# Two-layer encoder trunk: one projection block ahead of layer 1's second half, and the second half's first convolution pair starts on VectorE's own taps

## The chip, the cores and the metric

The kernel runs on one core of a Trainium2 chip, in fp32. The metric is the device time of one launch in microseconds (us), taken as the median of several runs. A profile shows one execution. The engines are named as in the profile: PE (TensorE matmul), PEld (its weight loads), DVE (VectorE), ACT (ScalarE), POOL (GpSimd) and SP (SyncE, which issues most DMAs).

## The reference

The input x has 1024 tokens of 1024 features. Every layer is x = x + mixer(RMSNorm(x)).

```
layer 0: h = rmsnorm(x); projections of h feed an S5 state-space layer with GLU (A)
         and a multi-scale retention (B), each times its own SiLU gate;
         x1 = x + concat(A, B) @ w_out            # 2048 -> 1024 features
layer 1: h1 = rmsnorm(x1)
         a, b, g = h1 @ w_c                        # three times 1024 features
         u = a * sigmoid(b)
         c = causal depthwise conv of u, 31 taps per feature, plus bias
         z = silu(layernorm over features(c)) * silu(g)
         x2 = x1 + z @ w_out_c
out = rmsnorm(x2)
```

Only layer 0's closing projection and layer 1 matter here.

## The kernel before, in words

**Tiling.** Data lies transposed: features on the 128 partitions, tokens along the free dimension. The 1024 tokens are two halves h = 0 and 1 of 512, the 1024 features 8 blocks nb of 128. Nearly every operation works on a tile of 128x512. A matrix product in fp32 is made of three passes in a faster type (`mm3`, L200 to L202): both operands are split into a high and a low part, and a product over 8 input blocks is 24 matmuls. The projection of layer 0 (`w_out`) has 16 input blocks, so 48 matmuls for a block of output. Its output tile is `mm_wo`; DVE adds the residual at L1418 and the sum of squares for the next norm follows (`square_sum`, "s1").

**Weights.** `plan` writes down the order in which weight blocks are used. A block is loaded by DMA (`wf`), cast by ACT to its high part (`wh`, L189), and POOL or DVE subtracts to make the low part (`wl`, L190). Each of `wf`, `wh` and `wl` has three buffers. For blocks needed in both halves, the low part is kept in device memory and loaded again for the second half (`wload_again`, L166).

**Layer 1.** `h1(h)` makes the normalized input in slices `h1h`/`h1l` (L1437 to L1441). `ab(h)` computes for each block the product b (`mm_b`), its tanh on ACT (`sb`, L1456), the product a (`mm_a`), and on DVE the gated `u` (L1469). `conv(h, n2)` computes the convolution of the pair of blocks n2 and n2+1. Of its 31 taps, ACT and POOL make the first few: ACT multiplies (L1502, L1506; tiles `tp`, three buffers), POOL adds (L1507). Unless the pair is `late`, ACT copies that partial sum into the accumulator in PSUM (L1513, two buffers), and DVE adds the other taps one by one, alternating between the two blocks (L1534). For a `late` pair, DVE starts with a multiply (L1531) and adds the partial sum ahead of the last tap (L1521). For the later pairs a pilot mean is subtracted before the last tap (L1523). L1614 to L1620 add the last block's outputs and squares into `cs` and `cq`, whose sums over features PE makes (`cst`, L509). From them the layer norm follows. `w_out_c` is the closing projection (`mm_oc`), with DVE's residual add at L1696 (x_0_0, x_1_0 and so on: block, half).

**Order.** The program's stages have priorities (`self.at(n)`: a lower number comes first), and a few edges are written by hand (`issue_after`). A scheduler with a timing model then fixes the order of instructions on each engine at build time. On the chip every engine runs its own list in order and waits on semaphores. So an edit in one stage can change the order in all later stages. The convolution taps of the first half's last pair beyond certain numbers (`NORM_TAP`) are held behind the second half's norm sum (L440).

Of the kernel before, what the change touches and what calls it, by code (L numbers as in the profile page):

```python
# [35 lines left out]
G0 = 3  # L36
# [10 lines left out]
def un(ap):  # L47

    return ap.rearrange("p (c a) -> p a c", a=LANES)


def nat(ap):

    return ap.rearrange("p (a c) -> p a c", a=LANES)
# [16 lines left out]
class Trunk:  # L71
# [22 lines left out]
    def plan(self):  # L94

        A = self.A

        seq = [(A["w_u01"][nb] if nb < 2 else A["w_ab"][nb], f"u{nb}") for nb in range(8)]
        seq += [(A["w_ab"][nb], f"g{nb}") for nb in range(8, 24)]
        for p in range(4):  # L100
            seq += [(A["w_ab"][28 + p], f"k{p}"), (A["w_ab"][24 + p], f"q{p}")]

            if p == 0:
                seq += [(A["w_v"][j], f"v{p}_{h}_{j}") for h in range(2) for j in range(4)]
            elif p > 1:
                seq += [(A["w_v"][2 * p + i], f"v{p}_{i}") for i in range(2)]
        self.ws_d = self.dram.tile([2, 2, P, 2, KB, P], F32, name="ws_d")
        quad = lambda i, j, m: A["w_glu"][i, m, :, j]
        sums = lambda n, m: self.ws_d[n // 2, m, :, n % 2]
        glu = [q for m in range(2) for q in (quad(0, 0, m), quad(0, 1, m))]  # L110
        glu += [q(m) for q in (lambda m: sums(0, m), lambda m: sums(2, m), lambda m: quad(1, 1, m)) for m in range(2)]
        glu += [sums(n, m) for m in range(2) for n in (3, 1)]
        seq += [(q, f"glu{i}") for i, q in enumerate(glu)]

        def wo(h):
            return [q for nb in range(8) for q in ((A["w_out"][nb], f"wos{nb}_{h}"),
                                                   (A["w_out"][8 + nb], f"wor{nb}_{h}"))]

        def ab(h):
            return [q for nb in range(8) for q in ((A["w_c"][8 + nb], f"cb{nb}_{h}"),  # L120
                                                   (A["w_c"][nb], f"ca{nb}_{h}"))]
        def cg(h, nbs):
            return [(A["w_c"][16 + nb], f"cg{nb}_{h}") for nb in nbs]
        seq += wo(0) + wo(1)[:4] + ab(0) + wo(1)[4:] + cg(0, range(G0)) + ab(1) + cg(0, range(G0, 8))
        seq += cg(1, range(G0))
        seq += [(A["w_out_c"][nb], f"woc{nb}_{h}") for h in range(2) for nb in range(8)]
        self.wseq, self.wissued, self.wgot = seq, {}, 0
        self.low_load, self.early_low = {}, None
        self.wnames, self.lo_d = {n for _, n in seq}, {}
# [1133 lines left out]
    def layer0_back_and_layer1(self, st):  # L1263
        nc, A = self.nc, self.A
        v, gp = nc.vector, nc.gpsimd
        lp = self.lp
# [139 lines left out]
        accs = {}  # L1406

        def w_out(h, nbs):
            for nb in nbs:
                xt = lp.tile([P, HALF], F32, name=f"xr{nb}_{h}", tag="ld", bufs=2)  # L1410
                nc.sync.dma_start(xt[:], A["xT"][nb, :, hs(h)])
                ws = self.wnext(f"wos{nb}_{h}")
                wr = self.wnext(f"wor{nb}_{h}")
                ps = self.bank(f"mm_wo{nb}_{h}", aux=False)
                seq = [(ws, ys[h], kb) for kb in range(KB)] + [(wr, yr[h], kb) for kb in range(KB)]
                self.gemm_seq(ps[:], seq, self.hold if h and nb == 0 else None)
                t = lp.tile([P, HALF], F32, name=f"x1_{nb}_{h}", tag="ev", bufs=3)
                v.tensor_tensor(nat(t[:]), un(ps[:]), nat(xt[:]), op=ALU.add)  # L1418
                nc.sync.dma_start(self.x1_d[rows(nb), hs(h)], t[:])
                if (nb, h) == (1, 1):  # L1420
                    self.later = lambda t=t: self.square_sum(lp, t, 1, 1, "s1", accs)
                else:

                    bank = (lambda: self.bank("s1q_bank")) if (nb, h) == (7, 1) else None
                    self.square_sum(lp, t, nb, h, "s1", accs, bank)
# [24 lines left out]
        def ab(h):  # L1450
            for nb in range(8):
                wb = self.wnext(f"cb{nb}_{h}")
                pb = self.bank(f"mm_b{nb}_{h}", aux=False)
                self.gemm(pb[:], wb, hx[h])
                sg = lp.tile([P, HALF], F32, name=f"sb{nb}_{h}", tag="ev", bufs=3)
                tanh = nc.scalar.activation(nat(sg[:]), un(pb[:]), AF.Tanh, scale=0.5)  # L1456

                with self.tc.issue_after(tanh.ins) if h == 0 and nb == 0 else nullcontext():
                    wa = self.wnext(f"ca{nb}_{h}")
                    if (nb, h) == (0, 0):  # L1460
                        self.later()
                pa = self.bank(f"mm_a{nb}_{h}", aux=False)
                self.gemm(pa[:], wa, hx[h])
                u = lp.tile([P, PADW + HALF], F32, name=f"u{nb}_{h}", tag="u", bufs=5)
                if h == 0:
                    gp.memset(u[:, :PADW], 0.0)
                else:
                    nc.scalar.copy(u[:, :PADW], tail[:, nb, :])
                v.scalar_tensor_tensor(nat(u[:, PADW:]), nat(sg[:]), 1.0, un(pa[:]), op0=ALU.add, op1=ALU.mult)  # L1469
                if h == 0:  # L1470
                    nc.scalar.copy(tail[:, nb, :], u[:, HALF:])
                ub[h][nb] = u
# [20 lines left out]
        def conv(h, n2):  # L1493


            accs_, outs, us, s0s = [], [], [], []
            late = h == 0 and n2 == 0
            for nb in (n2, n2 + 1):
                u = ub[h][nb]
                with self.at(105000 + 100000 * h + 100 * nb):  # L1500
                    s0 = lp.tile([P, HALF], F32, name=f"tp{nb}_{h}_0", tag="tp", bufs=3)
                    nc.scalar.activation(s0[:], u[:, 0:HALF], AF.Identity, scale=cw[:, nb, 0:1],  # L1502
                                         bias=self.vec(V_CB, nb))
                    for k in range(1, NT[h]):
                        sk = lp.tile([P, HALF], F32, name=f"tp{nb}_{h}_{k}", tag="tp", bufs=3)
                        nc.scalar.mul(sk[:], u[:, k:k + HALF], cw[:, nb, k:k + 1])  # L1506
                        gp.tensor_tensor(s0[:], s0[:], sk[:], op=ALU.add)  # L1507
                us.append(u)
                s0s.append(s0)
                acc = ps_cv.tile([P, HALF], F32, name=f"cv{nb}_{h}", tag="cv")  # L1510
                if not late:
                    with self.at(105000 + 100000 * h + 100 * nb):
                        nc.scalar.copy(acc[:], s0[:])  # L1513
                accs_.append(acc)
                outs.append(opB.tile([P, HALF], F32, name=f"co{nb}_{h}", tag="B0"))
            for k in range(NT[h], CONV_K):
                for i, nb in enumerate((n2, n2 + 1)):
                    dst = outs[i] if k == CONV_K - 1 else accs_[i]
                    tap = us[i][:, k:k + HALF], cw[:, nb, k:k + 1]
                    if k == CONV_K - 1 and late:  # L1520
                        v.tensor_tensor(accs_[i][:], accs_[i][:], s0s[i][:], op=ALU.add)  # L1521
                    if k == CONV_K - 1 and n2 >= 4:
                        v.tensor_tensor(accs_[i][:], accs_[i][:], pilot[h][:], op=ALU.subtract)  # L1523

                    if (h, nb, k) == (1, KB - 1, CONV_K - 1):
                        self.last_tap = *tap, accs_[i], dst
                        continue

                    ahead = (h, n2) == (0, 6) and k >= NORM_TAP[i]
                    if k == NT[h] and late:  # L1530
                        v.tensor_scalar(dst[:], *tap, None, op0=ALU.mult)  # L1531
                        continue
                    with self.tc.issue_after(self.norm_first.ins) if ahead else nullcontext():
                        v.scalar_tensor_tensor(dst[:], *tap, accs_[i][:], op0=ALU.mult, op1=ALU.add)  # L1534
            cv[h][n2:n2 + 2] = outs
# [213 lines left out]
        with self.at(100000):  # L1749
            w_out(0, range(8))  # L1750
            h1(0)
        self.hold = {4: self.last_stat}
        with self.at(200000):
            w_out(1, range(2))
            with self.at(110000):
                ab(0)
            w_out(1, range(2, 8))
            h1(1)
        self.norm_first = self.last_sum
        with self.at(300000):  # L1760
# [166 lines left out]
```

## Time and profile before

| | us |
|---|---|
| three runs | 1144.89, 1144.9, 1146.61; median 1144.9 |
| profiled execution | 1147.62, span 1145.8, mean granted PE clock 0.994 |
| busy: PE | 1123.9 (98% of the span) |
| busy: DVE | 853.5 (74%) |
| busy: POOL, ACT | 657.7 (57%), 488.2 (43%) |
| layer 1's second half begins (`r_R` on PE, first half's norm) | 709.65 |
| the convolution norm's sums of the second half (`cst` on PE) | 1074.00 |

Times in the trace count from the start of the span. PE's busy share of 98% is an average; the prediction looks at single stretches. A group's line names source line, engine, operation and tiles; in brackets behind an instruction stands how long its engine was idle before it and what ended that idle time.

### The profile page before, as it was taken

The numbers are of one execution on the slowest core, as the hardware profiler recorded it, in microseconds if no ns is written. First come the engines' busy times: TensorE is split into PE (matmuls) and PEld (weight loads), VectorE is DVE, ScalarE is ACT, GpSimd is POOL, SyncE is SP. The second block draws the span as 40 slices with busy tenths as digits, with TensorE's granted clock in tenths as the row PEclk, the third lists the DMA queues.
The fourth block names the chain that finished last, engine by engine and source line by source line (L and its number), as shares of the span: only waits on it lengthen the run. The fifth ranks groups of instructions, "written<-read, shape, count | busy, mean of one in ns | idle before, by whom it ended". The sixth has DMA issues, their size and how long they took to land.

```text
span 1145.8 us, 17197 instructions
## 1 busy us (share of the span) xinstructions
PE 1123.9 (98%) x6286; PEld 983.4 (86%) x6286; DVE 853.5 (74%) x1464; ACT 488.2 (43%) x719; POOL 657.7 (57%) x448
## 2 busy tenths in 40 slices
PE   9999999999999999999999999999999999999997
PEld 7888888888887888999887888888888888888787
DVE  6975798888417369596669632599999899999844
ACT  6423232223223321414446423545545676444674
POOL 2059999999235445333475111589544568678563
PEclk9999999999999999999999999999999999999999
DMA  9345355555487766858998998666778655357865
GB/s 352 113 129 159 128 166 177 162 175 177 154 256 247 285 199 211 297 182 308 382 375 295 321 321 285 191 232 203 247 249 298 238 177 173 120 188 248 287 226 193
DMA packets 117638, 261.46 MB, mean 228 GB/s; under 512 B 10673, under 2 KB 42289, under 8 KB 116913
## 3 DMA queue, kind: packets, MB, share of 16 engines
q1 hardware_dynamic: 117552, 260.36, 67.5%
q8 instruction: 49, 0.80, 0.3%
q14 instruction: 37, 0.30, 0.1%
HBM read 181.48 MB, written 74.65 MB: 224 GB/s over the span
## 4 chain that ended last, share of the span: by engine, by line
PE 34%; DVE 8%; DMA 7%; issue 2%; POOL 2%; ACT 1%; SPq 1%; POOLq 0%; ACTq 0%; DVEq 0%
DVE cv L1534 5%; PE mm_wo L202 5%; PE mm_wo L201 5%; PE mm_wo L200 5%; PE mm_b L201 2%; PE mm_b L202 2%; PE mm_b L200 2%; PE mm_a L202 2%; PE mm_a L201 2%; PE mm_a L200 2%; PE mm_oc L202 2%; PE mm_oc L201 1%; PE mm_oc L200 1%; DMA wf_glu<-w_glu 1%; DMA t_d<-th 1%
## 5 line engine op out<-in xcount | busy, mean ns | idle before, releaser
L1534 DVE SCALAR_TENSOR_TENSOR cv<-u,convw,cv 128x512 f32<-128x512 f32 x398 | 273.0, 749 | 6.6 <-ACT cv L1513 4.6
L1507 POOL TENSOR_TENSOR tp<-tp,tp 128x512 f32<-128x512 f32 x64 | 83.2, 1299 | 33.7 <-ACT tp L1506 32.7
L200 PE MATMUL mm_g<-xh,wh_g 128*128 128x512 f32 x256 | 98.9, 386 | 0.0
L201 PE MATMUL mm_g<-xl,wh_g 128*128 128x512 f32 x256 | 97.3, 380 | 0.0
L202 PE MATMUL mm_g<-xh,wl_g 128*128 128x512 f32 x256 | 97.2, 380 | 0.0
L437 POOL TENSOR_TENSOR s1q<-s1q,s1q 128x512 f32<-128x512 f32 x12 | 17.6, 1466 | 79.8 <-ACT s1q L432 79.8
L1506 ACT ACTIVATE tp<-u,convw 128x512 f32<-128x512 f32 x64 | 45.4, 718 | 35.5 <-POOL tp L1507 34.8
L200 PEld LDWEIGHTS mm_g<-xh,wh_g 128*128 128x128 f32 x256 | 48.4, 189 | 8.6 <-issue 1.2
L202 PEld LDWEIGHTS mm_g<-xh,wl_g 128*128 128x128 f32 x256 | 48.4, 189 | 6.9
L201 PEld LDWEIGHTS mm_g<-xl,wh_g 128*128 128x128 f32 x256 | 48.4, 189 | 6.8 <-issue 0.4
L190 POOL TENSOR_TENSOR wl_v<-wf_v,wh_v 128x1024 fp32r<-128x1024 f32 x12 | 31.0, 2593 | 36.4 <-ACT wh_v L189 36.4
L190 POOL TENSOR_TENSOR wl_glu<-wf_glu,wh_glu 128x1024 fp32r<-128x1024 f32 x14 | 34.3, 2447 | 29.9 <-ACT wh_glu L189 29.9
L200 PE MATMUL mm_oc<-zh,wh_woc 128*128 128x512 f32 (+1 forms) x144 | 51.3, 367 | 0.0
L202 PE MATMUL mm_oc<-zh,wl_woc 128*128 128x512 f32 (+1 forms) x144 | 51.0, 357 | 0.1
L201 PE MATMUL mm_oc<-zl,wh_woc 128*128 128x512 f32 (+1 forms) x144 | 51.1, 356 | 0.0
L201 PE MATMUL mm_u<-xl,wh_u 128*128 128x512 f32 x128 | 48.4, 381 | 0.7 <-DVE xl L316 0.7
L200 PE MATMUL mm_wo<-ysh,wh_wos 128*128 128x512 f32 x128 | 48.9, 382 | 0.0
L200 PE MATMUL mm_g<-h1h,wh_cg 128*128 128x512 f32 x128 | 48.9, 382 | 0.0
L201 PE MATMUL mm_b<-h1l,wh_cb 128*128 128x512 f32 x128 | 48.7, 381 | 0.1
L202 PE MATMUL mm_b<-h1h,wl_cb 128*128 128x512 f32 x128 | 48.7, 380 | 0.0
L201 PE MATMUL mm_wo<-ysl,wh_wos 128*128 128x512 f32 x128 | 48.5, 379 | 0.0
L202 PE MATMUL mm_wo<-ysh,wl_wos 128*128 128x512 f32 x128 | 48.5, 379 | 0.0
(526 smaller groups left out, 3622.9 us busy)
## 6 DMA issues: line engine op xcount, KB each, us to landing
wf_g<-w_ab SPq DMA_DIRECT2D x16, 512.0 KB
wf_wos<-w_out SPq DMA_DIRECT2D x16, 512.0 KB
wf_wor<-w_out SPq DMA_DIRECT2D x16, 512.0 KB
wf_cb<-w_c SPq DMA_DIRECT2D x16, 512.0 KB
wf_ca<-w_c SPq DMA_DIRECT2D x16, 512.0 KB
wf_woc<-w_out_c SPq DMA_DIRECT2D x16, 512.0 KB
wf_v<-w_v SPq DMA_DIRECT2D x12, 512.0 KB
wf_cg<-w_c SPq DMA_DIRECT2D x11, 512.0 KB
```

The lines of the kernel that those rows point to most:

```text
L190: self.low_made = lo[i].tensor_tensor(wl[:].rearrange(fl)[:, c], wf[:, c], h.bitcast(F32), op=ALU.subtract)
L200: nc.tensor.matmul(ps, wh[:, kb, :], xh, start=start, stop=False, **more)
L201: nc.tensor.matmul(ps, wh[:, kb, :], xl, start=False, stop=False, **more)
L202: self.last_mm = nc.tensor.matmul(ps, wl[:, kb, :], xh, start=False, stop=stop, **more)
L437: nc.gpsimd.tensor_tensor(a, a, sq[:], op=ALU.add)
L1506: nc.scalar.mul(sk[:], u[:, k:k + HALF], cw[:, nb, k:k + 1])
L1507: gp.tensor_tensor(s0[:], s0[:], sk[:], op=ALU.add)
L1534: v.scalar_tensor_tensor(dst[:], *tap, accs_[i][:], op0=ALU.mult, op1=ALU.add)
```

## The change

Before layer 1's products of the first half, one output block of layer 0's projection for the second half is computed instead of two; the other seven follow after. The weight order follows, and the square sum that is deferred into `ab(0)` is that of block 0. Besides, the first convolution pair (blocks 0 and 1) of the second half is treated as `late`, as that of the first half already was.

```
-        seq += wo(0) + wo(1)[:4] + ab(0) + wo(1)[4:] + cg(0, range(G0)) + ab(1) + cg(0, range(G0, 8))
+        seq += wo(0) + wo(1)[:2] + ab(0) + wo(1)[2:] + cg(0, range(G0)) + ab(1) + cg(0, range(G0, 8))
...
-                if (nb, h) == (1, 1):
-                    self.later = lambda t=t: self.square_sum(lp, t, 1, 1, "s1", accs)
+                if (nb, h) == (0, 1):
+                    self.later = lambda t=t: self.square_sum(lp, t, 0, 1, "s1", accs)
...
-            late = h == 0 and n2 == 0
+            late = n2 == 0
...
-            w_out(1, range(2))
+            w_out(1, range(1))
             with self.at(110000):
                 ab(0)
-            w_out(1, range(2, 8))
+            w_out(1, range(1, 8))
```

## The prediction

> **What bounds the kernel now.** I read the windows by stage first, then the waits of TensorE, then the timelines of VectorE and TensorE around the last wait. The windows give, for each stretch, the length and the busy time of PE, PEld, DVE, ACT and POOL, then the granted clock, the DMA share and GB/s.
>
> ```profile
> 900.00:940.00 40.00, 40.00 (x195) 35.17 (x194) 32.77 (x56) 28.58 (x42) 24.58 (x19) 1.00 0.64 223
> 940.00:1066.00 126.00, 126.00 (x585) 110.13 (x584) 125.82 (x193) 65.77 (x98) 96.44 (x68) 1.00 0.59 191
> 1066.00:1078.00 12.00, 9.31 (x32) 6.17 (x31) 9.81 (x15) 6.75 (x9) 7.93 (x5) 0.86 0.77 278
> 1078.00:1146.00 68.00, 61.06 (x333) 53.63 (x331) 33.37 (x61) 42.72 (x67) 34.90 (x31) 0.97 0.63 214
> ```
>
> PE is full from 900 to 1066 us, one matmul each 126.00/585 = 0.215 us. DVE is full from 940 to 1066 (125.82 of 126.00) and idle for 40.00 - 32.77 = 7.2 us between 900 and 940. Only in the third row does PE lose time, and the waits of PE name it:
>
> ```profile
> PE cst L509 <- DVE cs L1616: 2.7, 1, 2.7
> ```
>
> This is the second half's convolution norm: its sums over features (`cst`) need the last taps of the last convolution pair, which DVE computes one after the other. The timeline of DVE up to that point (start, length, engine, line, operation, output<-inputs):
>
> ```profile
> 1062.51 2.06 DVE L1534 SCALAR_TENSOR_TENSOR cv<-u,convw,cv 128x512 f32<-128x512 f32 x3
> 1064.48 0.69 DVE L1523 TENSOR_TENSOR cv<-cv,pilot 128x512 f32<-128x512 f32 x1
> 1065.08 0.74 DVE L1534 SCALAR_TENSOR_TENSOR cv<-u,convw,cv 128x512 f32<-128x512 f32 x1
> 1065.74 0.74 DVE L1534 SCALAR_TENSOR_TENSOR co<-u,convw,cv 128x512 f32<-128x512 f32 x1
> 1066.39 4.70 DVE L1534 SCALAR_TENSOR_TENSOR cv<-u,convw,cv 128x512 f32<-128x512 f32 x6
> 1071.13 0.70 DVE L1523 TENSOR_TENSOR cv<-cv,pilot 128x512 f32<-128x512 f32 x1
> 1071.94 0.70 DVE L1614 TENSOR_TENSOR cvs_bank<-cv,cs 128x512 f32<-128x512 f32 x1
> 1072.55 0.74 DVE L1615 SCALAR_TENSOR_TENSOR co<-u,convw,cv 128x512 f32<-128x512 f32 x1
> 1073.20 0.74 DVE L1616 SCALAR_TENSOR_TENSOR cs<-u,convw,cvs_bank 128x512 f32<-128x512 f32 x1
> 1073.86 0.68 DVE L1696 TENSOR_TENSOR x<-mm_oc,x1l 128x512 f32<-128x512 f32 x1
> ```
>
> Taps that alternate between the two blocks of a pair take (1064.48 - 1062.51)/3 = 0.66 us each; taps of one block that follow each other directly, each needing the one before, take (1071.13 - 1066.39)/6 = 0.79 us. From the L1523 at 1071.13 to the start of `cst` are 2.87 us. PE over the same stretch:
>
> ```profile
> 1070.93 0.38 PE L202 MATMUL mm_oc<-zh,wl_woc 128*128 128x512 f32 x1
> 1074.00 1.79 PE L509 MATMUL cst<-cs,ones 128*128 128x512 f32 x2 [2.69 <-DVE cs L1616]
> 1075.58 1.92 PE L509 MATMUL cst<-cq,ones 128*128 128x512 f32 x2
> 1076.51 1.39 PE L200 MATMUL mm_oc<-zh,wh_woc 128*128 128x512 f32 x1
> 1077.72 0.39 PE L201 MATMUL mm_oc<-zl,wh_woc 128*128 128x512 f32 x1
> ```
>
> The last product before `cst` is block 3 of the closing projection on the first half's tokens, ended at 1070.93 + 0.38 = 1071.31; `mm_oc` starts again behind `cst`. The wait has a second price. The two pairs of `cst` and the matmul behind them take 1077.72 - 1074.00 = 3.72 us, and the same form in mid-kernel, at full clock, is much quicker:
>
> ```profile
> 709.65 1.02 PE L509 MATMUL r_R<-s1q,ones 128*128 128x512 f32 x2
> 710.11 0.78 PE L200 MATMUL mm_wo<-ysh,wh_wos 128*128 128x512 f32 x1
> 710.72 0.38 PE L201 MATMUL mm_wo<-ysl,wh_wos 128*128 128x512 f32 x1
> ```
>
> One pair and one matmul are 1.07 us there, so two pairs and one matmul would be 1.07 + (1.07 - 0.215) = 1.92 us: 1.8 us lost. The clock of that stretch agrees:
>
> ```profile
> 1075.00:1080.00 5.00, 5.00 (x15) 3.31 (x15) 1.44 (x3) 3.70 (x7) 3.55 (x2) 0.73 0.96 333
> ```
>
> So the end is set by PE up to 1071.3, by DVE's taps up to 1074.0, and by PE again. A microsecond at `cst` reaches the end in full unless the 6.9 us of PE idle in the last windows row absorb it; those lie behind further matmuls, at the very end.
>
> **The sum's base.** The profiled execution took 1147.62 us with a span of 1145.8 (1.8 outside it); the three runs have a median of 1144.9. I take differences from the trace and put them on 1144.9. Of a measurement of this kernel, about 0.2% (2.3 us) can be told from no change.
>
> **Part one: one projection block ahead of layer 1 of the second half.** It removes no work: 48 matmuls, 48 x 0.215 = 10.3 us of PE, with their weights' casts and DMAs, the add at L1418 and the deferred square sum, go behind `ab(0)`. The risk is at the transition.
>
> ```profile
> 718.06 0.38 PE L202 MATMUL mm_wo<-yr1h,wl_wor 128*128 128x512 f32 x1
> ```
> ```profile
> 724.68 1.54 DVE L1441 SCALAR_TENSOR_TENSOR h1l<-xn,vecs,h1h 128x512 fp32r<-128x512 f32 x2
> 738.76 0.69 DVE L1418 TENSOR_TENSOR x<-mm_wo,xr 128x512 f32<-128x512 f32 x1 [12.55 <-PE mm_wo L202]
> 739.37 0.68 DVE L1469 SCALAR_TENSOR_TENSOR u<-sb,mm_a 128x512 f32<-128x512 f32 x1
> ```
>
> Block 0 ends there on PE (the next matmul can follow at 718.06 + 0.215 = 718.3); the normalized input `h1l` of layer 1 is complete only at 726.2, and the second block now fills that gap. In the changed kernel's instruction order PE works there on three products at once (b0, a0, b1), 9 matmuls or 1.94 us for each of the eight slices of `h1`, while DVE delivers a slice each 1.39 us (two of the last operations above, an add and a rescale at about 0.7). So the gap stays covered: 0. If only b0 stood there, it would end at 726.2 + 3 x 0.215 instead of 718.3 + 24 x 0.215 = 723.5: 3.4 us of wait.
>
> What is late next is a weight. b0, a0 and b1 hold all three weight buffers; the cast of the next block's a-weights can start only when b0 is done, 59 matmuls behind 718.3, at 731.0.
>
> ```profile
> 731.04 1.06 ACT L189 CAST wh_cb<-wf_cb 128x1024 fp32r<-128x1024 f32 x1 [5.61 <-PE mm_b L201]
> 732.11 1.28 ACT L1456 ACT_TABLE_LOAD   x1
> 733.41 0.60 ACT L1456 ACTIVATE sb<-mm_b 128x512 f32<-128x512 f32 x1
> ```
> ```profile
> 732.17 2.37 POOL L190 TENSOR_TENSOR wl_cb<-wf_cb,wh_cb 128x1024 fp32r<-128x1024 f32 x1 [5.66 <-ACT wh_cb L189]
> ```
>
> ACT does `sb` first (0.60), then the cast (1.06), then POOL the low part (2.37): 731.25 + 0.60 + 1.06 + 2.37 = 735.3. PE wants it after 76 matmuls, at 734.7. Cost about 0.7 us with hand-overs; from 0 (the two orders swap by a little) to 1.5 (the table load of 1.28 falls into it too). The first `u` comes about 7 us earlier than 739.37, and with it the first taps; but in the order 28 taps of the first half's last pair still stand behind the second half's norm sum (L440), as before, and that sum comes with PE's last projection block. DVE waits for it with nothing else to do, so this head start is worth 0 at the far end.
>
> **Part two: the second half's first pair adds the other engines' taps last.** The accumulator no longer waits for ACT's copy (L1513); DVE begins with a multiply (L1531, which replaces one L1534) and adds ACT's and POOL's partial sum before the last tap, two L1521.
>
> ```profile
> 912.08 0.69 DVE L1469 SCALAR_TENSOR_TENSOR u<-sb,mm_a 128x512 f32<-128x512 f32 x1 [1.70 <-PE mm_a L202]
> 915.74 3.13 DVE L1534 SCALAR_TENSOR_TENSOR cv<-u,convw,cv 128x512 f32<-128x512 f32 x4 [2.98 <-ACT cv L1513]
> ```
> ```profile
> L1521 DVE TENSOR_TENSOR cv<-cv,tp x2: 690/695/700, 767.3 to 779.2; 128x512 f32<-128x512 f32 x2
> ```
>
> Gain: most of DVE's 7.2 us of idle before 940, about 6.7. Cost: two adds, 2 x 0.6 = 1.2 us of issue. But the partial sums of this pair now hold two of the three `tp` buffers until their L1521, where before the copy freed them at once. ACT's second tap of block 2 (L1506) therefore waits for a DVE instruction near 950, and then follow its chain of ACT taps and POOL adds,
>
> ```profile
> L1507 POOL TENSOR_TENSOR tp<-tp,tp 128x512 f32<-128x512 f32 x64 | 83.2, 1299 | 33.7 <-ACT tp L1506 32.7
> ```
>
> four of 1.30 us plus an ACT tap each, with POOL's other work between. By the order I place block 2's copy at about 964 with DVE out of work from about 956: 7.9 us idle. The gain of 6.7 is spent there, and at the last `u` of the half DVE is level with before,
>
> ```profile
> 993.30 0.68 DVE L1469 SCALAR_TENSOR_TENSOR u<-sb,mm_a 128x512 f32<-128x512 f32 x1
> ```
>
> give or take 4 us, since the POOL chain is worked out and not seen.
>
> **What decides: where the add of block 3 stands.** Before, DVE's add of the closing projection's block 3 (L1696 at 1073.86) stood behind L1616, so nobody waited for it. In the changed order it stands ahead of the last 5 taps of the last block, of L1523, L1614, L1615 and L1616. It waits for the product that PE ends at 1071.31, and DVE takes its instructions in order. So `cst` starts no earlier than 1071.31 + 0.60 (the add's issue) + 5 x 0.79 + 2.87 = 1078.7, against 1074.0: **+4.7 us**. PE cannot deliver earlier: it has no gap from 900 to there. DVE's own count comes to the same place: from 993.30 to L1616 there are 125 instructions instead of 120, and 12 taps in direct succession instead of 6, so 1074.0 + 5 x 0.66 + 6 x (0.79 - 0.66) = 1078.1. Its 4 us of uncertainty count only upward, since the product's end is the floor. With the 0.7 of the weight stall, which moves that floor: **+5.4 us**. The clock's 1.8 us after the wait were paid before and are paid again; they could shrink at most to 0.
>
> PE's wait at `cst` grows from 2.69 to about 7.4 us. The Trainium skill (TensorE: Matmul & The Clock Gate, Part 1) says that the clock halves after an idle window of some 3.4 us and returns after a busy one, with windows that run freely. This trace half agrees: half speed came after only 2.69 us, and lasted about 3.5. By that rule the longer wait costs the same one window, or two if the first one is only partly busy.
>
> Forecast 1144.9 + 5.4, and 0.2 for the skew of DVE's own arrival: **1150.5 us**.
>
> **Rivals.**
> *A longer block-2 chain* (chance 0.18): DVE is late at the add of block 3 by 3 to 5 us because POOL serves the norm's multiplications between the adds. For it: POOL is 96.44 of 126.00 us busy from 940 on. Time 1153.5 to 1155.5.
> *A second half-speed window* (0.10): the matmuls behind `cst` run another 3.5 us at half speed, 1.8 us more, about 1152.3. For it: the wait is nearly three times as long. Against: one dip per wait in the trace before.
> *Uncovered transition* (0.05): PE waits at 718 to 726, 3.4 us, about 1153.9. Against: three products interleaved.
> *Faster* (0.06): DVE keeps its 6.7 - 1.2 = 5.5 us and the add of block 3 costs it nothing; the wait of 2.69 and the slow clock of 1.8 go, less the weight's 0.7: 1144.9 - 3.8 = 1141.1. It decides when DVE reaches that add with its product long done, about 7 us before `cst` is wanted. Against it: the product ends at 1071.31, directly before `cst` on PE. It could come true only if the adds of the tail did not run in the order that the program gives.
> *No change* (0.05): the change reaches `cst` but the 6.9 us of idle in the last windows row absorb it, 1143 to 1147. Against: PE is the engine that is late there.
>
> **How the numbers follow.** The forecast itself has 0.56, with a range of its own from 1148.5 (no weight stall, half of the clock's loss gone) to 1152.5. The range takes in the chain and the clock: 1148.0 to 1155.5; outside are the two rivals below and a little above. Faster by over 0.2%: 0.06; within: 0.05; slower: 0.89.
>
> **What would show it.** In the changed profile the wait `cst` <- `cs` L1616 should read 7 to 8 us; the L1696 before the last five taps should show an idle time ended by PE `mm_oc`, or start right behind 1072; L1513 of block 2 should start at 960 to 968 and DVE idle some 8 us before it; the idle at 909 to 925 should be gone; PE should wait 0 to 1.5 us for a `wl_ca` near 734. I am wrong if `cst` starts before 1077, if PE waits at 718 to 726, or if the end doesn't move with `cst`.

## The result, and the profile after

The changed kernel takes 1157.95 us (median of 4 runs, 1156.26 to 1160.19), the kernel before 1145.76 beside it: a ratio of 1.0101, 95% interval 1.0084 to 1.0118, so some 12 us slower. The forecast had the sign, and half of the size. The profiled execution took 1157.04, its span is 1155.3.

Where one profile is set against another, a shift has to be taken out first. Up to layer 0's closing projection the program is the same, yet that stretch alone varies by several us from one execution to the next:

```profile
621.16 0.38 PE L200 MATMUL mm_wo<-ysh,wh_wos 128*128 128x512 f32 x1
```
```profile
616.77 0.38 PE L200 MATMUL mm_wo<-ysh,wh_wos 128*128 128x512 f32 x1
```

The first row is the first `mm_wo` before, the second the same matmul after: 4.4 us earlier without any edit. I therefore compare the way from this matmul to the start of `cst` and from there to the span's end. Before it is 1074.00 - 621.16 = 452.8 and 71.8 us; after, 1082.97 - 616.77 = 466.2 and 72.3. All of the loss, 13.4 us, lies ahead of `cst`, and the profiles' spans differ by less only because of the early stretch.

PE's waits behind 700 us, after, as far as they are new or longer (engine, line, who is waited for: total, times, longest):

```profile
PE cst L509 <- DVE cs L1616: 7.6, 1, 7.6
PE cm L1545 <- POOL csr L1543: 3.7, 1, 3.7
PE r_R L509 <- DVE s1q L440: 1.4, 1, 1.4
PE mm_b L201 <- DVE h1l L1441: 1.1, 1, 1.1
```
```profile
PE mm_a L202 <- POOL wl_ca L190: 0.3, 1, 0.3
```

`cst` waits 7.6 us instead of 2.7, as forecast. The wait of `cm`, the pilot mean of the second half, was not forecast, and of the last three only the 0.3 was. DVE's timeline after, the taps that follow a wait for a copy, and the end of the taps:

```profile
962.02 3.13 DVE L1534 SCALAR_TENSOR_TENSOR cv<-u,convw,cv 128x512 f32<-128x512 f32 x4 [6.20 <-ACT cv L1513]
...
1012.70 16.56 DVE L1534 SCALAR_TENSOR_TENSOR cv<-u,convw,cv 128x512 f32<-128x512 f32 x25 [4.83 <-ACT cv L1513]
...
1034.05 12.61 DVE L1534 SCALAR_TENSOR_TENSOR cv<-u,convw,cv 128x512 f32<-128x512 f32 x19 [1.43 <-ACT cv L1513]
...
1070.15 5.50 DVE L1534 SCALAR_TENSOR_TENSOR cv<-u,convw,cv 128x512 f32<-128x512 f32 x7
1075.56 0.68 DVE L1696 TENSOR_TENSOR x<-mm_oc,x1l 128x512 f32<-128x512 f32 x1
1076.16 3.91 DVE L1534 SCALAR_TENSOR_TENSOR cv<-u,convw,cv 128x512 f32<-128x512 f32 x5
```

The wait of 6.2 at block 2 is the one that was worked out from the `tp` buffers (7.9). The other two are new; the only such wait behind the last `u` before was this one:

```profile
1004.03 23.14 DVE L1534 SCALAR_TENSOR_TENSOR cv<-u,convw,cv 128x512 f32<-128x512 f32 x35 [0.18 <-ACT cv L1513]
```

And the add of block 3 (L1696 at 1075.56) shows no idle time at all: DVE comes to it straight from its taps. PE shows how close that is:

```profile
1075.01 0.38 PE L202 MATMUL mm_oc<-zh,wl_woc 128*128 128x512 f32 x1
1082.97 2.08 PE L509 MATMUL cst<-cs,ones 128*128 128x512 f32 x2 [7.58 <-DVE cs L1616]
```

The product ended at 1075.01 + 0.38 = 1075.39. So two chains meet there within 0.2 us, PE's (late by its own waits) and DVE's (late by the copies). Which of them costs the time cannot be read from this profile alone.

The new waits have one kind of source. ACT and POOL around the wait at 1012:

```profile
1003.03 0.72 ACT L1506 ACTIVATE tp<-u,convw 128x512 f32<-128x512 f32 x1 [0.62 <-POOL tp L1507]
1003.66 0.58 ACT L1481 ACTIVATE sgg<-mm_g 128x512 f32<-128x512 f32 x1
1007.83 0.72 ACT L1506 ACTIVATE tp<-u,convw 128x512 f32<-128x512 f32 x1 [3.59 <-POOL tp L1507]
1009.93 0.81 ACT L1502 ACTIVATE tp<-u,vecs,convw 128x512 f32<-128x512 f32 x1 [1.38 <-POOL tp L1507]
1010.65 1.03 ACT L166 CAST wh_cg<-wf_cg 128x1024 fp32r<-128x1024 f32 x1
1011.59 0.59 ACT L1481 ACTIVATE sgg<-mm_g 128x512 f32<-128x512 f32 x1
1012.08 0.58 ACT L1513 COPY cv<-tp 128x512 f32<-128x512 f32 x1
```
```profile
1013.03 1.27 POOL L1667 TENSOR_TENSOR co<-gl,co 128x512 f32<-128x512 f32 x1 [3.13 <-DMA gl<-gs_d]
1014.25 1.27 POOL L1543 TENSOR_TENSOR csr<-cs,co 128x512 fp32r<-128x512 f32 x1
```

The copy that DVE waits for stands in ACT's queue behind the next blocks' taps, which wait for POOL. And `csr`, for which PE waits, stands behind POOL's multiply of a gate (L1667) that waits for its DMA. In the kernel before, `csr` stands ahead of that multiply:

```profile
1007.52 1.30 POOL L1543 TENSOR_TENSOR csr<-cs,co 128x512 fp32r<-128x512 f32 x1
...
1013.62 1.28 POOL L1667 TENSOR_TENSOR co<-gl,co 128x512 f32<-128x512 f32 x1 [1.44 <-DMA gl<-gs_d]
```

The engines are hardly busier than before (DVE 854.4 us against 853.5, POOL 656.6 against 657.7, ACT 488.2 in both); their queues hold things in another order. No run shows why that DMA lands as late as it does.

### The profile page after: what moved, and what is told of

Its sections match the earlier page's. It is cut to its first block, busy times and chain, and to the rows that moved or that the text cites. A ratio compares the mean times of both kernels' runs of the same rounds, so it can differ in the third digit from the quotient of the medians.

```text
span 1155.3 us, 17207 instructions
## 1 busy us (share of the span) xinstructions
PE 1124.7 (97%) x6286; PEld 984.0 (85%) x6286; DVE 854.4 (74%) x1466; ACT 488.2 (42%) x717; POOL 656.6 (57%) x448
## 4 chain that ended last, share of the span: by engine, by line
PE 68%; DVE 10%; DMA 10%; issue 4%; POOL 3%; ACT 2%; SPq 2%; POOLq 0%; DVEq 0%; ACTq 0%
PE mm_wo L201 5%; PE mm_wo L200 5%; PE mm_wo L202 5%; PE mm_g L200 4%; PE mm_g L201 4%; PE mm_g L202 4%; DVE cv L1534 4%; PE mm_a L202 2%; PE mm_a L200 2%; PE mm_a L201 2%; PE mm_b L201 2%; PE mm_b L202 2%; PE mm_b L200 2%; PE mm_oc L202 2%; PE mm_oc L200 2%
## 5 line engine op out<-in xcount | busy, mean ns | idle before, releaser
L190 POOL TENSOR_TENSOR wl_v<-wf_v,wh_v 128x1024 fp32r<-128x1024 f32 x12 | 31.0, 2587 | 36.7 <-ACT wh_v L189 36.7
L190 POOL TENSOR_TENSOR wl_glu<-wf_glu,wh_glu 128x1024 fp32r<-128x1024 f32 x14 | 33.8, 2411 | 31.2 <-ACT wh_glu L189 30.6
L202 PE MATMUL mm_g<-h1h,wl_cg 128*128 128x512 f32 x128 | 49.3, 385 | 0.0
L201 PE MATMUL mm_g<-h1l,wh_cg 128*128 128x512 f32 x128 | 49.2, 384 | 0.0
L202 PE MATMUL mm_a<-h1h,wl_ca 128*128 128x512 f32 x128 | 48.6, 380 | 0.3 <-POOL wl_ca L190 0.3
```

The lines of the kernel that those rows point to most:

```text
L190: self.low_made = lo[i].tensor_tensor(wl[:].rearrange(fl)[:, c], wf[:, c], h.bitcast(F32), op=ALU.subtract)
L201: nc.tensor.matmul(ps, wh[:, kb, :], xl, start=False, stop=False, **more)
L202: self.last_mm = nc.tensor.matmul(ps, wl[:, kb, :], xh, start=False, stop=stop, **more)
```

## The experiments

The times are medians, the ratios are against the kernel before on the same chip, with 95% intervals; "way" is first `mm_wo` to `cst` in the run's profile (before 452.8, changed 466.2).

**Which part does it?** Each part alone. In the first, only the line `late` goes back; in the second, only that line is changed.

```
 part1_only:  changed kernel, with  late = h == 0 and n2 == 0
 part2_only:  kernel before, with   late = n2 == 0
```

> Part one alone (one projection block ahead of layer 1; the second half's first pair keeps the copy). Theory T (two places): part one costs only the transition, r_R 1.4 + h1l 1.1 + wl_ca 0.3 = 2.8 us of waits, and part two the rest; here: no wait at cm, cst wait 2.7 to 3.5, time 3 to 4 us above before. Rival R (the earlier start of layer 1 is what reorders the second half): cm wait 3 to 4 and cst wait near 7 are here too, time 8 us or more above before.

> Part two alone (two blocks ahead as before; the second half's first pair adds the other engines' taps last). Theory T: no wait at 706 to 732, but the wait of cm on csr (3 to 4) and of cst on cs (7 to 8) both appear; time 9 to 11 us above before. Rival R: cst wait near 5 to 7 and no wait at cm, time about 5 us above before.

Part one alone: 1146.65 us, ratio 1.000 (0.998 to 1.0021); way 455.7. Its three waits at the transition are there (1.4, 1.1, 0.3), `cm` does not wait, `cst` waits 2.7. The 3 to 4 us did not show in the time. In the profile 2.9 us appear ahead of `cst`, and 2.0 come back behind it (69.8 us from `cst` to the end), because this time `cst` ran at full clock:

```profile
1073.53 1.13 PE L509 MATMUL cst<-cs,ones 128*128 128x512 f32 x2 [2.75 <-DVE cs L1616]
1074.49 1.02 PE L509 MATMUL cst<-cq,ones 128*128 128x512 f32 x2
```

That accounts for this one execution, not for the median: in the other nine the mean granted clock was 0.994 to 0.997, about as in the kernel before beside it (0.991 to 0.998). Whether part one costs any time stays open within the interval, some 2 us either way.

Part two alone: 1157.54, ratio 1.0077 (1.005 to 1.0104); way 463.6; waits of 4.5 at `cm` and 7.5 at `cst`. Theory T holds in the main: the two new orders come with part two alone, and part two carries most of the loss. By the ways, 2.9 and 10.8 us add up to 13.7, against 13.4 for both together.

**Does PE's wait at `cm` cost anything, and does the add of block 3?**

```
 csr_on_dve (changed kernel):
-  gp.tensor_tensor(sr[:], sm[:], cv[h][3][:], op=ALU.add)
+  (v if h else gp).tensor_tensor(sr[:], sm[:], cv[h][3][:], op=ALU.add)
 add3_behind (changed kernel): block 3's L1696 and what follows it are issued
 after the norm's last add, as block 4's already are
-  self.behind = {N0: self.squares_added}
+  self.behind = {N0 - 1: self.squares_added, N0: self.squares_added}; self.rest()
```

> The changed kernel with the last add of the pilot sum (csr, L1543) on VectorE for the second half instead of behind POOL's gate multiply, which waits for a DMA. Theory P (PE's chain sets cst alone): the cm wait of 3.7 and about 1.9 of half clock go, everything behind follows, the cst wait stays 7.6, time 5 to 6 us below the changed kernel. Theory C (a chain on DVE, 4.8 + 1.4 us of waits for ACT's copies L1513 and the taps behind, arrives at cst at the same time): the cm wait goes but the cst wait grows by as much, to 11 to 13 us; the end moves by less than 2.5 us.

> The changed kernel with only the add of block 3 (L1696) moved behind the norm's sums, where it stood before the change. Theory P, the step of the prediction (the add's place sets cst): cst follows 4 to 5 us earlier, time 4 to 5 us below the changed kernel. Theory C (DVE's chain of taps, late from its waits for ACT's copies, arrives there at the same time): only the add's own 0.6 us goes, with 0.1 for one more succession; cst waits 6.5 to 7.5 us, the way from the first mm_wo to cst is 465 to 466 us, time within 2 us of the changed kernel. csr and the wait at cm stay in both.

Without the wait at `cm`: 1158.71, ratio 1.0094 (1.006 to 1.0128), way 468.3. PE's waits of that run:

```profile
PE cst L509 <- DVE cs L1616: 11.6, 1, 11.6
PE mm_oc L202 <- POOL wl_woc L190: 1.7, 2, 1.5
PE r_R L509 <- DVE s1q L440: 1.4, 1, 1.4
PE mm_oc L200 <- DVE x L1696: 1.3, 1, 1.3
```

The wait moved from `cm` to `cst` and the end did not follow. The edit has side effects: DVE has one more add, its waits for copies behind 900 us rose from 12.5 to 14.5 us, which is about what the way grew, and PE waits 3.0 us at `mm_oc`. What it shows is theory C: without PE's 3.7 us and the slow clock behind them nothing is won, because DVE's chain is at least as late.

With the add of block 3 behind the sums: 1156.43, ratio 1.0106 (1.0076 to 1.0135), way 466.1 against 466.2. The taps that stood behind the add now run in one go, and end no earlier:

```profile
1067.37 9.46 DVE L1534 SCALAR_TENSOR_TENSOR cv<-u,convw,cv 128x512 f32<-128x512 f32 x12
1076.87 0.70 DVE L1523 TENSOR_TENSOR cv<-cv,pilot 128x512 f32<-128x512 f32 x1
```

This is theory C again: the add's place was no price by itself. With the wait at `cm` or with the add out of the way, DVE's chain still sets `cst`.

**All three orders put back.** `csr` on DVE, block 3's add behind, and ACT's copy of block 5 ahead of the fifth ACT tap of block 6:

```
 mend_three (changed kernel): the two edits above, and
+  with self.tc.issue_after(self.copies[5].ins) if (h, nb, k) == (1, 6, NT[h] - 1) else nullcontext():
       nc.scalar.mul(sk[:], u[:, k:k + HALF], cw[:, nb, k:k + 1])
```

> The changed kernel with three things put back in order: csr on VectorE, ACT's copy of block 5 (L1513) ahead of the fifth ACT tap of block 6, and the add of block 3 (L1696) behind the norm's sums. Theory C: the waits at cm and for the copy at 1012 go, cst waits 5 to 8 us for the taps that are left, time 4 to 7 us below the changed kernel, still 4 to 7 us above before (transition 2.8 and DVE some 3 us late from the tp buffers). Rival (the transition and the tp buffers carry it): less than 2 us below the changed kernel.

1157.23, ratio 1.0079 (1.005 to 1.0108), way 465.7. The wait of 4.8 near 1012 fell to 0.6, but the next copy, of block 6, now came 6.3 us late, behind a cast on ACT (L1259) that waits 5.3 us for POOL's next gate multiply:

```profile
1032.43 11.29 DVE L1534 SCALAR_TENSOR_TENSOR cv<-u,convw,cv 128x512 f32<-128x512 f32 x17 [6.29 <-ACT cv L1513]
```

By its time this is the rival's case, not the 4 to 7 us of gain that theory C gave: the late start is left, and shows at the next queue. Mending these three orders did not pay.

**Is it the buffers?** One experiment adds the suspected cost to the kernel before, one takes it from the changed kernel. `hold_only` keeps the copy, and a 128x1 add into scratch reads the two partial sums ahead of the last tap, so that their `tp` buffers are released as late as in part two. `early_release` adds the partial sum at tap 16 instead of ahead of tap 30.

```
 hold_only (kernel before):
+  if k == CONV_K - 1 and (h, n2) == (1, 0):
+      v.tensor_tensor(self.tiny[:], accs_[i][:, :1], s0s[i][:, :1], op=ALU.add)
 early_release (changed kernel); early_part2 (part two alone, same edit):
-  if k == CONV_K - 1 and late:
+  if k == (CONV_K - 1, 16)[h] and late:
       v.tensor_tensor(accs_[i][:], accs_[i][:], s0s[i][:], op=ALU.add)
```

> The kernel before with only the late release: the copy L1513 stays, but a tiny VectorE add (128x1, into scratch) reads the partial sums of blocks 0 and 1 of the second half just ahead of their last tap, so that their two tp buffers stay taken as long as in part two. Theory B (the buffers are the cause): DVE waits 5 to 8 us for block 2's copy near 960, PE waits 3 to 5 us at cm and 7 to 9 us at cst, time 9 to 14 us above before. Rival (the two full adds and the changed first tap are the cause): no such wait, time within 2 us of before.

> The changed kernel with one number changed: the second half's first pair adds the partial sum at tap 16 instead of ahead of the last tap (30), so its two tp buffers come free near 925 instead of 948 and 954. Theory B (the buffers' late release is the cause): DVE's wait of 6.2 near 960 is gone, cm waits 0 to 2, cst waits 0 to 3; time 8 to 13 us below the changed kernel, within 3 us of before. Rival (the order of the second half is fragile whatever the release): DVE and cst waits of 4 us or more are left, time 5 us or more above before.

> Part two alone with the add at tap 16 (two projection blocks ahead, as before). Theory B: DVE keeps some 5 us of the 6.7 that it idled before 925, cst waits 0 to 1.5 and keeps its clock; time 2 to 5 us below before. Rival (PE is bound elsewhere, by cm or by block 3's product): time within 1.5 us of before.

Hold alone: 1156.62, ratio 1.0094 (1.0068 to 1.0121), way 465.6, with 5.0 us of wait at `cm` and 7.6 at `cst`. Two tiny adds of 128x1, which keep the two buffers some 38 us longer, cost as much as part two. A miss in the detail: DVE does not wait 5 to 8 us near 960, it waits later and in five pieces:

```profile
DVE cv L1534 <- ACT cv L1513: 10.7, 5, 3.6
```

Of these, 6.8 us lie behind 990. On the chip itself only a small part of this is a wait for the tiny adds. From 940 to 975 us ACT's taps wait for

```profile
ACT tp L1506 <- DVE tiny L1524: 1.9, 1, 1.9
```

once (in the changed kernel 2.4 us for the two L1521), while `csr` has again moved behind the gate multiply. So the buffers act in two ways, as a wait and through the order that the scheduler then builds; no run separates the two. Nor was the same tiny add run without holding a buffer; the early release below, which keeps two full adds and loses nothing, speaks against the adds themselves.

Early release: 1145.93, ratio 0.9992 (0.9974 to 1.0011), way 452.8, as before the change. No wait at `cst` or `cm`, and DVE's waits for the copies behind 900 us are down from 12.5 in the changed kernel to

```profile
DVE cv L1534 <- ACT cv L1513: 3.0, 2, 2.3
```

One number in the source takes back the 12 us. Theory B is shown from both sides. Part two alone with it: 1144.70, ratio 0.9987 (0.9969 to 1.0004), way 451.7, `cst` waits 0.9. The forecast 2 to 5 us of gain are not shown; the interval reaches from 3.6 us of gain to half a us of loss.

**Is the copy needed?** A first tap that reads the partial sum itself takes DVE's wait out of ACT's queue.

```
 no_copy_changed, no_copy_before; no_copy_half2 (kernel before, h == 1 only);
 no_copy_mended (changed kernel, with csr on DVE and block 3's add behind);
 early_no_copy (early_part2, h == 1 only):
-  nc.scalar.copy(acc[:], s0[:])
-  v.scalar_tensor_tensor(dst[:], *tap, accs_[i][:], op0=ALU.mult, op1=ALU.add)
+  v.scalar_tensor_tensor(dst[:], *tap, (s0s if k == NT[h] else accs_)[i][:], op0=ALU.mult, op1=ALU.add)
```

> The changed kernel without ACT's copies L1513: VectorE's first tap reads the partial sum from SBUF itself, so it waits for POOL and not for a place in ACT's queue. Theory Q (behind the buffers it is ACT's queue: the copies stand behind taps and casts that wait for POOL, and POOL for a DMA): DVE's waits of 4.8 and 1.4 near 1012 and 1033 go, the 6.2 near 960 shrinks by no more than 1, no wait at cm; cst waits 4 to 7 us; time 5 to 8 us below the changed kernel, 4 to 7 above before. Rival (POOL itself is late, wherever the sum is read): DVE waits as long for POOL, time within 2 us of the changed kernel.

> The changed kernel without the copies, with csr on VectorE and the add of block 3 behind the norm's sums. Theory Q: as without copies alone, less 0 to 2 us, since these two waits no longer decide; still 3 to 6 above before because of block 2's buffers. Rival (block 3's add still decides): 3 us or more below the run without copies alone.

> The kernel before without the copies L1513 (the same edit). Theory Q: the copies cost DVE 2.98 + 1.05 us at 915 and 925; without them 1 to 2 of it stay as waits for POOL, cst is wanted 1 to 3 us earlier, its wait falls to 0 to 2 and may keep the full clock; time 1 to 4 us below before. Rival (a tap that reads two SBUF inputs is slower beside POOL and the buffers are held longer): time the same or up to 3 us above.

> The kernel before without the copies L1513 in the second half only. If the 5.8 us that the run without any copies lost came from the first half (PE's wait of 3.3 for the norm sum L440 and the slow clock behind it): no wait at r_R, cst waits 0 to 1.5; time 0 to 4 us below before. Rival (it came from the second half): time 3 us or more above before, with waits at cm or cst.

> Part two alone with the add at tap 16 and without the second half's copies: both gains together. Theory B: cst waits 0 to 1; time as early part two or up to 2 us below it. Rival (cm then waits for csr behind POOL's gate multiply): cm waits 2 to 5 us and nothing is won over early part two.

On the changed kernel: 1155.35, ratio 1.0078 (1.0051 to 1.0105), way 461.0; DVE's waits at 1012 and 1033 are gone, the one of 6.2 stays and is now one for POOL:

```profile
964.15 0.76 DVE L1534 SCALAR_TENSOR_TENSOR cv<-u,convw,tp 128x512 f32<-128x512 f32 x1 [6.22 <-POOL tp L1507]
```

So `cst` comes 5.2 us earlier on its way, in line with theory Q: the two waits that went were 4.83 and 1.43. But `cm` still waits 1.8, where none was expected, and the median's 2.6 us below the changed kernel's are fewer than the 5 to 8 expected. Mended besides: 1154.47, ratio 1.0071 (1.0045 to 1.0097), way 460.8: nothing more, so neither block 3's add nor the wait at `cm` decides here either.

On the kernel before it is a loss: 1151.95, ratio 1.0051 (1.0033 to 1.0069). Theory Q missed this. PE waits 3.3 us for the second half's norm sum near 880, ahead of which DVE now is late. In the second half only: 1148.22, ratio 1.0019 (1.0005 to 1.0033); the first half explains most of the loss, not all; `cst` waits 3.7 (2.7 before) and `cm` 1.4, so no gain is left in the second half by itself. With the early release: 1144.31, ratio 0.9986 (0.9967 to 1.0005), way 450.2, no wait at `cst`: the fastest version, its interval far below the changed kernel's, and from the kernel before not told apart.

## Why the prediction failed

**What bounds the kernel: right.** `cst` behind DVE's last taps is where all of the difference comes out, and it reached the end nearly one to one (13.4 us ahead of `cst`, 0.5 behind, so the slow clock was paid again with a little on top, and no second full window of it).

**Part one, 0.7 us: too small.** The waits sum to 2.8. The 0 for `h1l` was 1.1; the weight's 0.7 was 0.3; and the 1.4 at `r_R` was not seen. That one is a collision, below. In time, part one alone cannot be told from no change.

**Part two, "level with before" at the last `u`: right.** The wait of 7.9 at block 2 was 6.2. The last `u` came 990.95 - 616.77 = 374.2 us behind the first `mm_wo`, before 993.30 - 621.16 = 372.1: 2.1 later, which is less than the transition's 2.8.

```profile
990.95 0.69 DVE L1469 SCALAR_TENSOR_TENSOR u<-sb,mm_a 128x512 f32<-128x512 f32 x1
```

**What decides, the add of block 3: the step that failed.** The floor of +4.7 is sound arithmetic (`cst` started 7.6 us after the product's end, forecast 7.4), but two things in this step were wrong. The product itself came 458.6 us behind the first `mm_wo` instead of 450.2: "PE cannot deliver earlier" was right, that it would deliver on time was not, as it waited 2.8 at the transition and 3.7 at `cm`, with half speed behind that (matmuls 0.43 us apart from 1016.46 to 1019.45). And the place of the add does not set `cst`: the idle time ahead of the add, which the prediction had named as a sign, is not there, and with the add moved away `cst` comes no earlier (466.1 against 466.2), since DVE's chain is as late without it.

The sum should have followed DVE's chain past the last `u`. There it counted instructions (5 more and 6 more successions, 4.1 us) and took the waits for copies as unchanged. They grew from 0.18 to 4.83 + 1.43 = 6.26 us, by 6.1, because the copies stand in ACT's queue behind taps that wait for POOL. Counted from the last `u`, that is the missing term: 2.1 + 4.1 + 6.1 = 12.3 of the 13.4. The run without copies bears out its size, with `cst` 5.2 us earlier. That the 4 us of uncertainty "count only upward" was true, but the room for it was set too small.

**The rival "longer block-2 chain" came nearest**, with DVE late through POOL's chain at 3 to 5 us and a chance of 0.18; part two's text had named the held buffers. It looked for the price at block 2, where the waits were even shorter than forecast; the price came 50 us later. The wait of `cm` behind a gate multiply was in neither. It is real, and it cost nothing in the runs where DVE was as late.

**Part two's gain** exists: with the early release `cst` doesn't wait. The kernel has little to win there: the wait was 2.7 us, and its slow clock comes and goes.

## What to carry to other kernels

When an edit keeps a buffer longer, follow its pool, not the edited instructions: here 128x1 adds that hold two of three buffers some 38 us longer cost nearly as much as the whole change, and an earlier release takes all of it back, within the noise. In a kernel whose queues are ordered at build time by a timing model, one delay moves instructions in other queues, so read every queue that the critical engine waits for until the wait that ends the path, not to the first one that looks sufficient. If two chains meet at one point, price both and move one of them by itself before calling it the cause.

## What the runs showed of the hardware

A VectorE add with two SBUF inputs waited for a GpSimd operation that ran beside it. L440 took 0.69 us before. After, it takes 2.36, and ends 0.55 us behind POOL's subtraction of a weight that part one brought to this place:

```profile
708.33 0.69 DVE L440 TENSOR_TENSOR s1q<-s1q,s1q 128x512 f32<-128x512 f32 x1 [0.76 <-ACT s1q L432]
```
```profile
703.95 2.36 DVE L440 TENSOR_TENSOR s1q<-s1q,s1q 128x512 f32<-128x512 f32 x1 [0.76 <-ACT s1q L432]
```
```profile
703.40 2.36 POOL L190 TENSOR_TENSOR wl_cb<-wf_cb,wh_cb 128x1024 fp32r<-128x1024 f32 x1 [8.45 <-ACT wh_cb L189]
```

703.40 + 2.36 = 705.76 is POOL's end, 703.95 + 2.36 = 706.31 that of L440, and PE's `r_R` waited 1.4 us for it. This `r_R`, near 707, waits 1.4 us in all eight kernels here that have part one, and not at all in the seven without it. The Trainium skill (SBUF — State Buffer, "SBUF: two separate sides") states this as an exclusive lock: of a DVE operation with two SBUF inputs and a GpSimd operation that reads SBUF, the second one stands still until the first has ended. These rows agree. The taps, with one input in PSUM, show no such effect at 0.73 to 0.78 us each; in the run without copies on the kernel before, the 14 first taps with both inputs in SBUF took 0.75 to 2.85 us, the longest of them beside POOL's subtraction of a weight (L190).

A wait of PE of the same length did and didn't halve the clock: 2.69 us before (two pairs of `cst` and a matmul in 3.72 us), 2.75 in part one alone (full clock). After 7.58 us half speed lasted 4.9 us, from 1082.97 to 1087.83, where the steps between matmuls fall from 0.43 us to 0.26:

```profile
1087.40 0.63 PE L202 MATMUL mm_oc<-zh,wl_woc 128*128 128x512 f32 x1
1087.83 0.42 PE L200 MATMUL mm_oc<-zh,wh_woc 128*128 128x512 f32 x1
1088.09 0.38 PE L201 MATMUL mm_oc<-zl,wh_woc 128*128 128x512 f32 x1
```

The free-running windows of some 3.4 us that the Trainium skill describes (TensorE: Matmul & The Clock Gate, Part 1) fit the 4.9, between one window and two, but its rule of one idle window is not strict: waits shorter than that halved the clock in one execution and not in another. Between these two executions it makes some 2 us (71.8 and 69.8 from `cst` to the end).
